# One paced sequence for four token mixers in a decoder block on one Trainium2 core

## The chip, the cores and the metric

The kernel runs on one core of one Trainium2 chip. The metric is the device time of one execution in microseconds (us), given as the median of the runs. The engines are named as the profile names them: PE (TensorE, matrix products; PEld is its weight load), DVE (VectorE), ACT (ScalarE), POOL (GpSimd) and SP (SyncE). In this kernel POOL and SP do little but issue transfers.

## The reference

One decoder layer over 2048 positions of width 1024, float32. A condition vector gives shifts, scales and gates. The first sub-layer projects the normalised input once, feeds two groups of mixers with the result, joins their outputs in one projection and adds it to the residual. The second sub-layer is a feed-forward with a causal convolution of width 3.

```python
sh1, sc1, g1, sh2, sc2, g2 = jnp.split(silu(c) @ w_ada + b_ada, 6)
h = rms_norm(x, norm1_g) * (1 + sc1) + sh1
gq, gk, gv, gr, glr, aq, ak, av = split(h @ w_in)
y_gla = gla_group(gq, gk, gv, log_a, gr, gla_norm_g)        # 4 heads, chunked, a running state
y_att = dilated_attention_group(qa, ka, av)                 # 8 heads, (window, dilation) = (128,1), (512,4), (2048,16)
x = x + g1 * (concat([y_gla, y_att]) @ w_out)
h = rms_norm(x, norm2_g) * (1 + sc2) + sh2
u_gate, u_val = split(causal_depthwise_conv(h @ w_up) + conv_b)
x = x + g2 * ((silu(u_gate) * u_val) @ w_down)
```

## The kernel before

The 2048 positions are four chunks of 512 (`NCH = 4`, `T = 512`). A chunk passes through four pieces of work. `proj(c)` is the input projection; its results go to DRAM scratch. `mix(c)` reads them back and runs the mixers: `gla(c, 0)` and `gla(c, 1)`, then `attn(c, hp)` for four pairs of heads, hp = 0 to 3. `outproj(c)` reads the mixers' output, projects it and computes the second norm. `ffn(c)` is the feed-forward: 44 blocks of the up-projection, and the down-projection in groups of four feature tiles.

Every dense product is made of triples of matmuls (`mm3`, L306 to L308), because each float32 operand is split into a high and a low part. They write to a pool of four PSUM banks called `psg`. The mixers, and every small product of the other pieces (the norms' sums at L442 and L445, the q and k norms at L500 and L501, the gate at L612 and L624), write to a second pool of four banks called `psa`. A weight block is loaded into `wraw` by POOL, rounded by ACT (L240) and its remainder taken by DVE (L241).

The code of one attention pair (two heads, L830 to L972), in the order of its steps, is: scores of dilation 16 (PE L865, biased and reduced to a maximum by DVE L836), scores of dilations 4 and 1 (PE L830, DVE L836), 24 exponentials (ACT L840, after their negated maximum by DVE L855), a weighing of the three branches in some fifteen small DVE operations with two small products (PE L897 and L921), scaling of the probabilities (DVE L917 and L928), 40 transposes on PE (L850) that ACT (L181) and DVE (L183) copy out, products with the values (PE L949 and L954), a last scaling (DVE L934), a transpose back (PE L969), a copy (ACT L971), a sum (DVE L972) and the store. One pair follows the other: the next begins at L865 behind the L969 of the pair ahead. The tiles `kt`, `kw` and `v16` of a pair share two buffers, so the next pair's `kw` is loaded once L949 has read `v16`.

Each piece is a Python generator that yields after a step. `beside(a, na, b, nb)` runs through b and, after each step of b, as many steps of a as keep the share na/nb. `along` does the same and yields, `chain` joins generators. `mix(c)` has 68 steps. `gemm` is the projection of all chunks together with the late part of the condition's product (`ada_late`). This writing order gives each instruction its priority. The scheduler then orders every engine's instructions by priority and by when they can start in its own timeline, and hands out a pool's banks in the order in which the code asks for them.

In the second half of an `outproj(c)`, after its eight blocks and the norm's sum, stands `self.tail`: the last group of the down-projection of the chunk ahead (for chunk 0, the last block of the projection of chunk 3). It is dense work for PE while the second norm is applied.

Of the kernel before, what the change touches and what calls it, by code (L numbers as in the profile page):

```python
# [21 lines left out]
NCH = 4  # L22
# [78 lines left out]
def beside(a, na, b, nb):  # L101

    acc = 0.0
    done = object()
    for _ in b:
        acc += na / nb
        while acc >= 1.0:
            acc -= 1.0
            if next(a, done) is done:
                acc = -1e9  # L110
    for _ in a:
        pass


def along(a, na, b, nb):

    acc = 0.0
    done = object()
    for _ in b:
        acc += na / nb  # L120
        while acc >= 1.0:
            acc -= 1.0
            if next(a, done) is done:
                acc = -1e9
        yield
    for _ in a:
        pass


def chain(*gs):  # L130
    for g in gs:
        yield from g


class K:
# [945 lines left out]
    def run(self):  # L1081
        self.ada_setup()
        self.scratch()
        self.x1, self.h2, self.tail = {}, {}, ()
        self.planned = False
        xs = self.load_x(0)
        acc = None
        for k in range(5):
            acc = self.square(acc, xs[k])
        sqs = [self.tmp.tile([P, T], F32, name="sq", bufs=3) for _ in range(5, KD)]  # L1090
        for sq, x in zip(sqs, xs[5:]):
            self.nc.scalar.activation(sq, x, AF.Square)
        rstd = {0: self.norm_end(acc, more=sqs)}
        h0, ws, done = [], {}, {b: self.pg() for b in FIRST}
        spare = self.at.tile([P, 2048], F32R, name="w0", tag="kt", bufs=2)
        ring = self.at.tile([P, 2048], F32, name="ring", tag="kt", bufs=2)
        for k in range(KD):
            big = [self.at.tile([P, 1024], F32, name="wada", tag="big", bufs=4)]
            pair = [self.gp.tile([P, T], F32, name="wada", tag=t) for t in ("ghi", "glo")] if k < 5 else [ring[:, (k - 5) * 1024:(k - 4) * 1024] if k < 7 else self.at.tile([P, 1024], F32, name="wada", tag="v4", bufs=1)]
            gs = [self.ada(KD + k, big), self.ada(k, pair)]  # L1100
            for g in gs:
                next(g)
            if k < len(FIRST):
                b = FIRST[k]
                ws[b] = self.wblock(self.A["w_ch"][b], KD, P, spare if k == 3 else None)
            for g in gs:
                next(g, None)
            if k == GATE:
                self.gate_ins = self.last
            h0.append(self.norm_mod1(xs[k], k, rstd[0], self.G1, self.mod[:, 0:8]))  # L1110
        for b in FIRST:
            for k in range(KD):
                self.mm3(done[b], ws[b][k:k + 1], h0[k:k + 1], k == 0, True)
        self.consts()

        def src(c):
            def f(k):
                t = self.tmp.tile([P, T], F32, name="sq", bufs=3)
                ld = self.dq.dma_start(t, self.A["xT"][c, k])
                if c == 1:  # L1120
                    self.after(ld)
                return t
            return f

        self.wleft, self.wready, self.wpos = list(self.plan()), [], 0
        self.planned = True
        hs = [h0]

        def begin(c):
            hs.append(self.norm_mod(src(c), rstd[c], self.G1, self.mod[:, 0:8]))  # L1130

        def proj(c):
            yield from self.proj(c, hs.pop(), (lambda: begin(c + 1)) if c < 3 else None, () if c else done)

        def stats(c):

            acc = None
            xs = [src(c)(0)]
            yield
            for k in range(KD):  # L1140
                if k + 1 < KD:
                    xs.append(src(c)(k + 1))
                yield
                acc = self.square(acc, xs[k], xs[k])
            yield
            rstd[c] = self.norm_end(acc, split=True)
            yield

        def ahead(c):

            return along(stats(c), 11, proj(c - 1), 18)

        gemm = along(self.ada_late(), 66, chain(ahead(1), ahead(2), ahead(3), proj(3)), 94)
        for _ in range(27):
            next(gemm)
        beside(self.mix(0), 68, gemm, 72)
        beside(self.mix(1), 68, chain(self.outproj(0), self.ffn(0)), 90)
        beside(self.mix(2), 68, chain(self.outproj(1), self.ffn(1)), 86)
        beside(self.mix(3), 68, chain(self.outproj(2), self.ffn(2)), 90)
        for _ in chain(self.outproj(3), self.ffn(3)):  # L1160
            pass


# [59 lines left out]
```

## Time and profile before

| what | us |
|---|---|
| median of 2 runs | 2602.16 |
| the runs | 2600.97 and 2603.35 |
| span of the profiled execution | 2603.1 |
| first mixer's first DVE step (L663) | 184.0 |
| first eviction of the output projection (L1005), chunks 0 to 3 | 689.7, 1197.9, 1697.8, 2199.5 |
| end of `attn(c, 3)` (L972 starts), chunks 0 to 3 | 663.9, 1160.8, 1635.6, 2153.6 |

The profiled execution's span is within the range of the runs' times. The stages follow from the third and fourth entries: until 184 us start and the projection of chunk 0; until 690 us the rest of the projection with the mixers of chunk 0; then three stages of output projection and feed-forward, each with the mixers of the next chunk; and from 2200 us the last chunk's, with no mixers beside it.

A busy share of PE counts a matmul from its start to its modelled end. Matmuls overlap, so a share near 100% says that PE never stood empty for long, and the rate is read from the spacing of starts.

### The profile page before, as it was taken

Reading aid. Unit: us, or ns where it says so; the run is one execution under the profiler, and the core shown is the slowest. Engines: PE = TensorE matmul, PEld = TensorE weight load, DVE = VectorE, ACT = ScalarE, POOL = GpSimd, SP = SyncE. Lnnn points to the kernel's source line nnn. Section 1 sums busy time; section 2 is a strip of 40 time slices with the busy share of each in tenths; the row PEclk is TensorE's granted clock in tenths of the full one; section 3 lists DMA queues with packets and bytes.
Section 4 is the critical chain, followed back from the end, with each engine's and each line's share of the span. In section 5 each row is a group of like instructions: output and inputs, shape, how many; then the busy total and the mean of one; then the engine's idle time right before and its main releaser. Section 6 shows DMA issues by size and latency. Waiting matters only on the chain.

```text
span 2603.1 us, 46834 instructions
## 1 busy us (share of the span) xinstructions
PE 2559.7 (98%) x18142; PEld 2104.0 (81%) x18142; DVE 1930.2 (74%) x4091; ACT 1277.7 (49%) x2626; POOL 444.4 (17%) x816
## 2 busy tenths in 40 slices
PE   5999999999999999999999999999999999999999
PEld 4888888788788888887788888878888888788887
DVE  7578877768788777777987777689777775766665
ACT  4566556656454444454545544346445453433332
POOL 1343332313210000012100000310000003100001
PEclk8999999999999999999999999999999999999999
DMA  8766675756633344455334344733443435432322
GB/s 291 242 226 234 211 236 170 239 167 201 230 108 100 123 128 122 127 174 199 123 96 139 117 134 136 252 131 114 129 140 127 143 103 189 150 103 97 96 96 84
DMA packets 164194, 405.13 MB, mean 156 GB/s; under 512 B 19154, under 2 KB 61956, under 8 KB 162692
## 3 DMA queue, kind: packets, MB, share of 16 engines
q0 software_dynamic: 88128, 308.59, 35.5%
q1 hardware_dynamic: 75844, 93.55, 11.6%
q8 instruction: 143, 2.34, 0.4%
q14 instruction: 79, 0.65, 0.1%
HBM read 339.15 MB, written 62.91 MB: 154 GB/s over the span
## 4 chain that ended last, share of the span: by engine, by line
PE 77%; issue 1%; DVE 1%; DMA 1%; ACT 0%; POOL 0%; POOLq 0%; DVEq 0%; ACTq 0%
PE psg L306 22%; PE psg L307 22%; PE psg L308 22%; PE psa L850 2%; PE psa L830 2%; PE psa L954 2%; PE psa L680 1%; PE psa L949 1%; PE psa L865 0%; PE psa L753 0%; PE psa L752 0%; PE psa L969 0%; DMA wada<-in_w_ada_dram 0%; PE psa L757 0%; PE psa L779 0%
## 5 line engine op out<-in xcount | busy, mean ns | idle before, releaser
L306 PE MATMUL psg<-hhi,whi 128*128 128x512 f32 x1992 | 782.0, 396 | 9.2 <-ACT hhi L467 5.3
L307 PE MATMUL psg<-hlo,whi 128*128 128x512 f32 x1992 | 782.9, 394 | 6.7 <-DVE hlo L469 6.5
L308 PE MATMUL psg<-hhi,wlo 128*128 128x512 f32 x1992 | 780.2, 392 | 0.7 <-DVE wlo L241 0.7
L240 ACT CAST whi<-wraw 128x1024 fp32r<-128x1024 f32 (+1 forms) x391 | 410.4, 1051 | 467.4 <-PE psg L307 363.2
L241 DVE TENSOR_TENSOR wlo<-wraw,whi 128x1024 fp32r<-128x1024 f32 (+1 forms) x391 | 478.0, 1223 | 187.2 <-ACT whi L240 181.5
L306 PEld LDWEIGHTS psg<-hhi,whi 128*128 128x128 f32 x1992 | 375.0, 189 | 95.2 <-ACT hhi L467 9.3
L307 PEld LDWEIGHTS psg<-hlo,whi 128*128 128x128 f32 x1992 | 375.3, 188 | 86.7 <-DVE hlo L469 9.6
L308 PEld LDWEIGHTS psg<-hhi,wlo 128*128 128x128 f32 x1992 | 375.5, 188 | 80.6 <-issue 1.7
L306 PE MATMUL psg<-ghi,whi 128*128 128x512 f32 x744 | 295.1, 398 | 0.0
L307 PE MATMUL psg<-glo,whi 128*128 128x512 f32 x744 | 292.1, 393 | 0.5 <-DVE glo L999 0.5
L308 PE MATMUL psg<-ghi,wlo 128*128 128x512 f32 x744 | 291.6, 392 | 0.0
L234 POOL DMA_DIRECT2D wraw<-in_w_up_dram x176 | 93.6, 532 | 982.6 <-DVE wlo L241 850.5
L1073 DVE SCALAR_TENSOR_TENSOR x<-psg,mod,x 128x512 f32<-128x512 f32 x192 | 143.2, 749 | 118.2 <-PE psg L308 115.7
L306 PE MATMUL psg<-whi,hhi 128*128 128x512 f32 (+2 forms) x512 | 172.8, 345 | 8.3 <-ACT stg L523 6.2
L308 PE MATMUL psg<-whi,hlo 128*128 128x512 f32 (+2 forms) x512 | 174.8, 345 | 0.0
L307 PE MATMUL psg<-wlo,hhi 128*128 128x512 f32 (+2 forms) x512 | 174.6, 343 | 0.1
L306 PEld LDWEIGHTS psg<-ghi,whi 128*128 128x128 f32 x744 | 139.5, 188 | 34.0 <-issue 5.3
L307 PEld LDWEIGHTS psg<-glo,whi 128*128 128x128 f32 x744 | 139.8, 188 | 30.0 <-issue 1.9
L308 PEld LDWEIGHTS psg<-ghi,wlo 128*128 128x128 f32 x744 | 139.7, 188 | 29.5 <-issue 0.7
L840 ACT ACTIVATE big<-big,nm 128x256 f32<-128x256 f32 (+1 forms) x256 | 122.4, 480 | 33.6 <-DVE nm L855 33.4
L1028 ACT ACTIVATE y<-psg,tables_sb 128x512 f32<-128x512 f32 x176 | 136.1, 776 | 4.5 <-PE psg L308 3.2
L1029 DVE SCALAR_TENSOR_TENSOR y<-psg,tables_sb,y 128x511 f32<-128x511 f32 x176 | 130.7, 743 | 3.7 <-ACT y L1028 3.6
(253 smaller groups left out, 3621.9 us busy)
## 6 DMA issues: line engine op xcount, KB each, us to landing
wraw<-in_w_up_dram POOLq DMA_DIRECT2D x176, 512.0 KB, 3.6
wraw<-in_w_down_dram POOLq DMA_DIRECT2D x88, 512.0 KB, 3.6
wraw<-in_w_ch_dram POOLq DMA_DIRECT2D x44, 512.0 KB, 4.3
v<-v SPq DMA_DIRECT2D x68, 256.0 KB, 5.6
wada<-in_w_ada_dram POOLq DMA_DIRECT2D x64, 256.0 KB, 4.8
wraw<-in_w_tokw_dram POOLq DMA_DIRECT2D x32, 512.0 KB, 4.2
wraw<-in_w_out_dram POOLq DMA_DIRECT2D x32, 512.0 KB, 4.7
sq<-in_xT_dram POOLq DMA_DIRECT2D x48, 256.0 KB, 4.9
```

The lines of the kernel that those rows point to most:

```text
L234: self.dq.dma_start(raw[:, :n], src)
L240: nc.scalar.copy(hi[:, :n], raw[:, :n])
L241: nc.vector.tensor_tensor(lo[:, :n], raw[:, :n], hi[:, :n].bitcast(F32), op=ALU.subtract)
L306: nc.tensor.matmul(ps, wh, hh, start=first and k == 0, stop=False, skip_group_check=shared)
L307: nc.tensor.matmul(ps, wh, hl, start=False, stop=False, skip_group_check=shared)
L308: self.lastmm = nc.tensor.matmul(ps, wl, hh, start=False, stop=k == n - 1, skip_group_check=shared)
L830: nc.tensor.matmul(at(i, hh, z), q[H[hh], i * P:(i + 1) * P], key(H[hh], i, z), start=True, stop=True, skip_group_check=True)
L840: nc.scalar.activation(t[:, lo:hi], t[:, lo:hi], AF.Exp, bias=nm[:, hh, g, i:i + 1], scale=2.0 ** -(h + 1), accum_out=dn[:, hh, g, i:i + 1])
L850: nc.tensor.transpose(ps[:n, i * P:(i + 1) * P], part(S[hh], i), self.C("id"))
L1028: nc.scalar.activation(y, ps, AF.Identity, bias=self.cb[:, b:b + 1], scale=self.cw[:, 2, b:b + 1])
L1029: nc.vector.scalar_tensor_tensor(y[:, 1:], ps[:, :T - 1], self.cw[:, 1, b:b + 1], y[:, 1:], op0=ALU.mult, op1=ALU.add)
L1073: nc.vector.scalar_tensor_tensor(x1, ps, self.mod[:, 40 + cb:41 + cb], x1, op0=ALU.mult, op1=ALU.add)
```

## The change

Before, each chunk's mixers ran beside a piece of dense work of their own: those of chunk 0 beside the rest of the projection, and those of chunk c+1 beside the output projection and feed-forward of chunk c, with 68 steps to 72, 90, 86 and 90. Now the 272 steps of all four chunks' mixers are one sequence, written beside the rest of the projection and the output projection and feed-forward of chunk 0, with 272 steps to 157. Behind it, the output projections and feed-forwards of chunks 1, 2 and 3 are written without any mixers. No instruction is added or removed.

```diff
         for _ in range(27):
             next(gemm)
-        beside(self.mix(0), 68, gemm, 72)
-        beside(self.mix(1), 68, chain(self.outproj(0), self.ffn(0)), 90)
-        beside(self.mix(2), 68, chain(self.outproj(1), self.ffn(1)), 86)
-        beside(self.mix(3), 68, chain(self.outproj(2), self.ffn(2)), 90)
-        for _ in chain(self.outproj(3), self.ffn(3)):
+        beside(chain(*(self.mix(c) for c in range(NCH))), 272, chain(gemm, self.outproj(0), self.ffn(0)), 157)
+        for _ in chain(self.outproj(1), self.ffn(1), self.outproj(2), self.ffn(2), self.outproj(3), self.ffn(3)):
             pass
```

The scheduler's order decides what this does to each engine. The first place is the end of the last attention pair, `attn(3, 3)`, on PE. Names with `psg` are dense products, names with `psa` are the mixers' and the norm's. Before, the end of that pair stands between dense triples of the feed-forward of chunk 2:

```order
L850 MATMUL psa<-consts_sb,big 128x128 x4
L306 MATMUL psg<-hhi,whi 128x512
L307 MATMUL psg<-hlo,whi 128x512
L308 MATMUL psg<-hhi,wlo 128x512
L949 MATMUL psa<-v_21968,s_21923 32x64 x16
L949 MATMUL psa<-v_21968,s_21924 32x64 x16
L954 MATMUL psa<-big,v_22097 64x4x32 x16
L954 MATMUL psa<-big,v_21878 64x8x16 x16
L969 MATMUL psa<-consts_sb,pt 128x128 x4
L306 MATMUL psg<-hhi,whi 128x512
```

Now no dense row stands in the whole pair, nor in the pair ahead of it, and the sum of the second norm of chunk 1 (L445) stands behind both:

```order
L897 MATMUL psa<-xm,consts_sb 128x64
L850 MATMUL psa<-consts_sb,s_15939 128x128 x4
L850 MATMUL psa<-consts_sb,s_15940 128x128 x4
L921 MATMUL psa<-xm,consts_sb 128x32
L850 MATMUL psa<-consts_sb,big 128x128 x32
L949 MATMUL psa<-v_15984,s_15939 32x64 x16
L949 MATMUL psa<-v_15984,s_15940 32x64 x16
L954 MATMUL psa<-big,v_16071 64x4x32 x16
L954 MATMUL psa<-big,v_15918 64x8x16 x16
L969 MATMUL psa<-consts_sb,pt 128x128 x4
L445 MATMUL psa<-rstd,ones 128x512
L306 MATMUL psg<-hhi,whi 128x512 x4
```

What moved is the dense work: counted in dense matmuls between the L969 of one pair and the next, there were 212 to 252 for each of the last three pairs of a chunk's mixers before (chunks 1 to 3); for `attn(3, 1)` there are now 119, for `attn(3, 2)` and `attn(3, 3)` none. The feed-forward of chunk 1 begins behind the last mixer, and 5,136 of the 9,792 dense matmuls stand behind it.

The second place is DVE at the same end. Before, the last pair's evictions (L183, L934, L972) stand between the feed-forward's weight remainders (L241) and convolution (L1029 to L1045):

```order
L183 COPY big<-psa 128x4x128
L241 TENSOR_TENSOR wlo<-wraw,whi 128x1024
L1029 SCALAR_TENSOR_TENSOR y_22474<-psg,tables_sb,y_22474 128x511
L1032 SCALAR_TENSOR_TENSOR y_22474<-halo,tables_sb,y_22474 128x1
L934 TENSOR_TENSOR pt<-psa,f 128x512
L1030 SCALAR_TENSOR_TENSOR y_22474<-psg,tables_sb,y_22474 128x510
L1033 SCALAR_TENSOR_TENSOR y_22474<-halo,tables_sb,y_22474 128x2
L1040 SCALAR_TENSOR_TENSOR th<-th,y_22474 128x512
L972 TENSOR_TENSOR stage<-psa,stage 128x16x32
```

Now the pair has DVE to itself, and behind it come the eight tiles of the second norm (L465, L469):

```order
L917 TENSOR_SCALAR big<-big,f 128x256 x8
L923 TENSOR_TENSOR xm<-psa,consts_sb 128x32
L924 TENSOR_REDUCE f<-xm 128x2x4
L928 TENSOR_SCALAR big<-big,f 128x256 x8
L183 COPY big<-psa 128x4x128 x4
L934 TENSOR_TENSOR pt<-psa,f 128x512
L972 TENSOR_TENSOR stage<-psa,stage 128x16x32
L465 SCALAR_TENSOR_TENSOR sq<-x,G_111,rstd 128x512 x3
L469 SCALAR_TENSOR_TENSOR hlo<-sq,mod,hhi 128x512 x2
```

The third place is PE at `attn(1, 2)`, from the weighing of its branches (L921) on. Before, its transposes (L850) alternate with the up-projection of chunk 0:

```order
L306 MATMUL psg<-hhi,whi 128x512
L921 MATMUL psa<-xm,consts_sb 128x32
L850 MATMUL psa<-consts_sb,big 128x128 x12
L307 MATMUL psg<-hlo,whi 128x512
L308 MATMUL psg<-hhi,wlo 128x512
```

Now the pair runs where the projection of chunk 3 ends, without a dense row until its L969. The sums of the projection's last norm of q or k (L500, L501) stand in the middle of its transposes, and the dense rows that follow (`ghi`) belong to the output projection of chunk 0:

```order
L921 MATMUL psa<-xm,consts_sb 128x32
L850 MATMUL psa<-consts_sb,big 128x128 x16
L500 MATMUL psa<-sqr,blk 128x512
L501 MATMUL psa<-sqr,blk 128x512
L850 MATMUL psa<-consts_sb,big 128x128 x16
L949 MATMUL psa<-v_8619,s_8574 32x64 x16
L949 MATMUL psa<-v_8619,s_8575 32x64 x16
L954 MATMUL psa<-big,v_8741 64x4x32 x16
L954 MATMUL psa<-big,v_8510 64x8x16 x16
L969 MATMUL psa<-consts_sb,pt 128x128 x4
L306 MATMUL psg<-ghi,whi 128x512
```

What moved is again the dense work. Between the L969 of one pair and that of the next there are 42 dense matmuls for `attn(0, 2)`, 128 for `attn(1, 0)` and 48 for `attn(1, 2)` now; before, 234, 239 and 252 (the counts of first pairs run from the last transposes of the gated linear attention, L779). PE passes between dense rows and other rows 669 times before and 503 times now.

## The prediction

> **What bounds the kernel now.** I read the page first, its busy times and its slices.
>
> ```profile
> PE 2559.7 (98%) x18142; PEld 2104.0 (81%) x18142; DVE 1930.2 (74%) x4091; ACT 1277.7 (49%) x2626; POOL 444.4 (17%) x816
> DVE  7578877768788777777987777689777775766665
> PEclk8999999999999999999999999999999999999999
> ```
>
> PE is busy throughout, DVE between 0.6 and 0.9. Then the busy time by stage (busy us of PE, PEld, DVE, ACT and POOL, then granted clock, DMA share and GB/s), cut at the marks of the table above:
>
> ```profile
> 184.00:690.00 506.00, 501.26 (x4155) 419.65 (x4154) 395.71 (x922) 309.76 (x672) 162.31 (x289) 1.00 0.65 216
> 690.00:1198.00 508.00, 508.00 (x3814) 415.87 (x3813) 377.94 (x796) 245.44 (x553) 57.75 (x108) 1.00 0.41 133
> 1198.00:1698.00 500.00, 497.55 (x3840) 405.79 (x3839) 385.75 (x887) 241.67 (x546) 60.92 (x114) 1.00 0.44 142
> 2200.00:2603.10 403.10, 396.16 (x1734) 325.92 (x1732) 263.35 (x402) 145.63 (x180) 48.10 (x90) 0.99 0.32 105
> ```
>
> The same view for the `psa` products alone:
>
> ```profile
> 1198.00:1698.00 500.00, 95.46 (x2070) 80.34 (x2070) 71.58 (x192) 26.06 (x74) 1.00 0.44 142
> ```
>
> A stage with mixers is about 100 us longer than the last, which has none, and the mixers' products keep PE busy for 95 us of it. So PE is the bound in every stage, and the mixers cost their own PE work and little else: everything they wait for is hidden behind dense matmuls. That cover is what the change redistributes.
>
> **Engine sums do not decide.** Since no instruction is added or removed, PE's sum stays. The packed stretch (184 us to the end of the feed-forward of chunk 0) takes over the mixers of two more chunks. On PE it would need 506 + 508 + 2 x 100 = 1214 us. One chunk's mixers put 385.75 - 263.35 = 122 us on DVE and 241.67 - 145.63 = 96 us on ACT, so DVE would have 396 + 378 + 245 = 1019 us (84%) and ACT 748 us (62%). No engine is full on average. What decides is how fast the one chain of mixer steps can go, and whether PE has dense rows while it waits for it.
>
> **Rate of that chain.** The ends of two successive pairs, `attn(2, 0)` and `attn(2, 1)`:
>
> ```profile
> 1436.94 1.07 DVE L972 TENSOR_TENSOR stage<-psa,stage 128x512 f32<-128x512 f32 x1 [0.77 <-ACT stage L971]
> ...
> 1501.08 1.06 DVE L972 TENSOR_TENSOR stage<-psa,stage 128x512 f32<-128x512 f32 x1 [2.88 <-ACT stage L971]
> ```
>
> A pair takes 64 us there with 212 dense matmuls beside it. Dense matmuls start every 0.227 us (first two rows below), which is 48 us; the other 16 us are the pair's own on PE.
>
> ```profile
> 510.80 0.39 PE L307 MATMUL psg<-wlo,hhi 128*128 128x512 f32 x1
> 511.03 0.39 PE L308 MATMUL psg<-whi,hlo 128*128 128x512 f32 x1
> ...
> 513.59 0.49 PE L306 MATMUL psg<-whi,hhi 128*128 128x512 f32 x1 [1.49 <-ACT stg L550]
> ...
> 515.42 0.63 PE L307 MATMUL psg<-wlo,hhi 128*128 128x512 f32 x1
> 515.85 0.63 PE L308 MATMUL psg<-whi,hlo 128*128 128x512 f32 x1
> ```
>
> Where the new order leaves 143 to 205 dense matmuls per pair, PE has 49 to 63 us of work for each. How long would a pair take with nothing else on the engines? That is a sum along its chain:
>
> ```profile
> L954 PE MATMUL psa<-big,v 128*64 128x128 f32 x944 | 55.1, 274 | 0.0
> L971 ACT COPY stage<-psa 128x512 f32<-128x512 f32 x16 | 16.8, 1052 | 35.7 <-PE psa L969 35.7
> L972 DVE TENSOR_TENSOR stage<-psa,stage 128x512 f32<-128x512 f32 x16 | 17.1, 1067 | 21.6 <-ACT stage L971 20.9 <-DMA kw<-kn 0.8
> L836 DVE CUSTOM_DVE_ANT_0 s<-psa,consts_sb 128x32 f32<-128x32 f32 (+3 forms) x128 | 22.0, 236 | 0.8 <-PE psa L865 0.8
> L840 ACT ACTIVATE s<-s,nm 128x32 f32<-128x32 f32 (+3 forms) x128 | 44.5, 349 | 32.0 <-DVE nm L855 32.0
> L840 ACT ACTIVATE big<-big,nm 128x256 f32<-128x256 f32 (+1 forms) x256 | 122.4, 480 | 33.6 <-DVE nm L855 33.4
> L894 DVE TENSOR_TENSOR xm<-md,consts_sb 128x64 f32<-128x64 f32 x16 | 3.6, 224 | 35.6 <-ACT big L840 33.4 <-ACT halo L1035 2.1
> L917 DVE TENSOR_SCALAR big<-big,f 128x256 f32<-128x256 f32 (+1 forms) x128 | 33.0, 333 | 0.0
> L928 DVE TENSOR_SCALAR big<-big,f 128x256 f32<-128x256 f32 (+1 forms) x128 | 34.6, 345 | 0.3
> L183 DVE COPY big<-psa 128x512 f32<-128x512 f32 (+1 forms) x60 | 40.3, 676 | 5.7 <-PE psa L850 5.6
> ```
>
> From one pair's value products on: L954 55.1/16 = 3.4 us, the transpose back 0.6 (an estimate from the four it has), L971 1.05, L972 1.07 (DVE's order puts it ahead of the next scores), eight maxima of 0.24, 1.9, and the next few with their scale, 0.9: 8.9 us. Then 24 exponentials on ACT, 8 x 0.35 + 16 x 0.48 = 10.5 us. Then the weighing, some fifteen small DVE operations at L894's 0.22, 3.3 us, and a copy, 0.7. Then L917 and L928, eight each, (33.0 + 34.6)/16 = 4.2 us, and four copies L183 of the last transposes, 2.7 us. That is 30.3 us, and some 2.5 us for two dozen hand-overs and L949 (estimate): 33 us. It is an estimate from durations alone; the other bound is the 64 us just read, with all the dense work in the way. I take a value near the lower end because in the rows now at the end (first and second places above) nothing else stands on PE and DVE.
>
> One thing adds to it. After PE waited 1.49 us at 513.59, matmuls start 0.43 us apart instead of 0.227: the granted clock is halved. An uncovered pair leaves PE idle through the exponentials, so its products would run at half the clock; those on the chain (L954, the last transposes, the first scores) are about 5 us and would add 4. I take 37 us for an uncovered pair.
>
> The Trainium skill, "TensorE: Matmul & The Clock Gate", Part 1, says that the clock halves after at least one idle window of about 3.4 us and returns after a busy window of that length. The trace agrees with the return (0.43 us spacing from 514 to 518) but shows the drop after a wait of 1.49 us. By the page the uncovered pairs would pay the same, since their exponentials leave PE 10 us, and the sum stays; by the row, each short wait of (2) can cost 1.7 us more, half of the 3.4 us at half rate, which their upper bound holds.
>
> **The change, part by part.** (1) The end of the mixers. The dense work of chunk 1's output projection and tail runs out when `attn(3, 1)` is at L921. The feed-forward of chunk 1 needs the norm's sum L445, for which the pool gives a bank only behind the last mixer. So PE has: the rest of that pair, 6 us (copies 2.7, products, L928); two uncovered pairs, 74 us; from the last L949 to the first dense matmul the 5 us of L954, L969 and L971, then the norm as the trace has it on ACT and DVE, below: 2237.18 - 2230.29 = 6.9 us, and 2 us more at half clock, together 14 us.
>
> ```profile
> 2230.29 1.28 ACT L447 ACT_TABLE_LOAD   x1
> ...
> 2237.18 0.47 PE L306 MATMUL psg<-hhi,whi 128*128 128x512 f32 x1 [1.46 <-ACT hhi L467]
> ```
>
> In the last stage of before this norm ran beside the tail and left PE 1.46 us of wait; here the tail is used up. The window is 6 + 74 + 14 = 94 us, and 2.3 pairs x 16 = 37 us of it is PE work that was paid before too: **+57 us**. With 30 us a pair it is +43, with 47 us +77.
>
> (2) Earlier stretches where the projection waits for a bank of `psa` in turn and the four of `psg` are full. `attn(0, 2)` has 42 dense matmuls (10 us) and 48 belong to `attn(1, 2)` (11 us); with 14 to 16 us of their own PE has 24 to 27 us for a chain of 33 to 37 us: 10 us lost in each. `attn(1, 0)` has 128, but none until its L897: the maxima and exponentials, 3 + 10.5 and hand-overs, some 16 us, against 5 us of scores: 11 us. Together **+31 us**, from 0 (a chain of 25 us) to 60 (contended).
>
> (3) Elsewhere in the packed stretch DVE carries 84%, and the first pair and the first gated attention of a chunk run beside q and k norms and weight remainders. The slices at 0.8 and 0.9 of DVE cost PE next to nothing before, so I give it **+15 us**, from 0 to 50.
>
> (4) PE passes between dense and other rows 166 times less. A matmul's 0.39 exceeds its spacing of 0.227 by 0.16 us, the most that a pass can cost; half of it, **-13 us**, from 0 to -27.
>
> (5) Transfers: the mixers' loads keep their number and move on SP's queue only, with their own pair; the DMA share is 0.41 to 0.44 where they get denser, and 0.65 beside the projection. I cost them at nothing; the chain of an uncovered pair covers them. If `kw`, loaded behind L949, came late, it would show as a wait of L830 on DMA and is inside the 47 us bound. The three later stages lose 30% of their transfers and DVE work, and PE, at 98% and more there before, gains nothing.
>
> Sum on the profiled span: 2603.1 + 57 + 31 + 15 - 13 = 2693. The median of the runs is 0.9 us under that span, so **2692 us**, 3.5% slower.
>
> **Rivals.** A: the same or faster, not slower. If an uncovered pair ran at its busiest engine (the exponentials, 11 us of ACT, and evictions; some 22 us) rather than along its chain, (1) would be 6 + 44 + 14 - 37 = +27, (2) and (3) nothing, (4) -13: 2617 us, no change that can be told. It turns at about 29 us a pair: (1) +41, (2) +10, (3) +10, (4) -13, just under 2% of 2602. For it: PE ran at full rate before, so the order left the chain slack. Against: the exponentials cannot start before their maxima, nor the scaling before all of them. Chance 0.12.
>
> B: the chain is contended everywhere. If each of the 24 pieces of mixers (16 pairs, 8 gated attentions) ended 6 us later than its dense work lasts, since DVE is at 84% and first in its queue may be a 1.2 us weight remainder, (3) is 24 x 6 = 144 us: 2821 us. For it: the packed pairs have 49 us where they had 64. Against: the two slices of DVE at 9 tenths and the many at 8 were borne before with PE full. Chance 0.08.
>
> C: the clock. If the half clock doubled all 37 us of PE work in the window and some 15 us in the places of (2), 2692 + 52 - 8 (already counted) = 2736 us. For it: the wait at 513.59. Against: most products run while ACT or DVE is the later one. Chance 0.12.
>
> That the mixers would not leave the later feed-forwards is excluded by the order: the last mixer stands ahead of 5,136 dense matmuls.
>
> **How the numbers follow.** The forecast, 2650 to 2735, has 0.68, A 0.12, B 0.08, C 0.12. The range reaches from 2635, with a part of A, to 2765 with C and the upper bounds of (1) and (2), and leaves out B and the rest of A. A change of 2% (52 us) is about what a measurement of this kernel can tell from none: slower by over 2% takes the forecast, B and C, less 0.02 for its lower edge, 0.86; within 2% 0.13; faster 0.01, since nothing here gives more than (4).
>
> **What would show it.** Right: a slice or two of low PE at about 1420 us (the 975 us of dense work ahead, 370 of mixers, 44 of start and 33 of (2) to (4)), with the exponentials on ACT beside it; a gap of some 37 us between the last two L972; a halved clock there; three stages of about 400 us behind it with PE at 98% and more and DVE near 0.65. The norm's part is right if the first dense matmul comes 10 to 14 us behind the last L969. Step (2) is shown by PE waiting around 500 to 750 us. Wrong: PE full at the end of the mixers; or PE waits spread over all pairs (B).

## The result and the profile after

The changed kernel takes 2755.28 us (median of 2 runs, 2753.97 to 2756.59) against 2602.16 before: ratio 1.0589, 95% interval 1.0558 to 1.0619. It is slower by 153 us. The forecast was 2692 us, 63 us less. The time lies above the forecast's own band, 2650 to 2735, and inside the range, 2635 to 2765, by 10 us. The profiled execution has a span of 2754.8 us, 151.7 more than that of before, and the sums below are made against it.

The slices of the page, 69 us each:

```profile
PE 2623.9 (95%) x18142; PEld 2152.9 (78%) x18142; DVE 1943.2 (71%) x4091; ACT 1278.9 (46%) x2624; POOL 443.6 (16%) x816
PE   6999988999889999999998699999999999999999
DVE  7688875796776987669876576666576666676665
PEclk8999998999899999999999799999999999999999
```

Behind the start, PE is below 9 tenths in three places: around 410 us, around 760 us and around 1530 us. The first two lie beside the projection, the third is the end of the mixers. Busy times by stage (PE, PEld, DVE, ACT, POOL, granted clock, DMA share, GB/s):

```profile
184.00:470.00 286.00, 270.85 (x2510) 224.87 (x2509) 219.22 (x566) 159.19 (x394) 77.69 (x139) 0.96 0.57 192
470.00:560.00 90.00, 80.22 (x815) 65.83 (x814) 69.93 (x191) 56.68 (x137) 20.16 (x36) 0.91 0.58 193
...
680.00:850.00 170.00, 149.76 (x1286) 118.65 (x1285) 115.71 (x391) 99.69 (x275) 32.48 (x58) 0.88 0.54 177
...
1488.00:1574.00 86.00, 55.08 (x716) 46.85 (x715) 50.32 (x200) 39.35 (x122) 3.31 (x6) 0.82 0.43 129
1574.00:1955.00 381.00, 380.26 (x1670) 314.21 (x1671) 245.46 (x380) 145.09 (x219) 50.27 (x95) 1.00 0.32 111
1955.00:2355.00 400.00, 398.38 (x1746) 328.36 (x1744) 258.66 (x397) 154.05 (x230) 59.80 (x112) 1.00 0.35 121
```

From 1574 us on the kernel is what the prediction said it would be: PE full, DVE at 0.65, full clock. Everything that was lost was lost before. For the same 18142 matmuls PE's busy time rose by 64 us, from 2559.7 to 2623.9, and its empty time by 87. The window at the end, from PE's order of time:

```profile
1488.19 0.39 PE L308 MATMUL psg<-ghi,wlo 128*128 128x512 f32 x1
1488.42 0.30 PE L921 MATMUL psa<-xm,consts_sb 128*128 128x32 f32 x2
...
1508.86 2.95 PE L830 MATMUL psa<-kw,qn 64*128 64x256 f32 x15
1520.02 0.69 PE L897 MATMUL psa<-xm,consts_sb 128*128 128x64 f32 x2 [8.21 <-DVE xm L894]
...
1566.57 0.66 PE L969 MATMUL psa<-consts_sb,pt 128*128 128x128 f32 x4
1567.06 1.02 PE L445 MATMUL psa<-rstd,ones 128*128 128x512 f32 x2
1573.81 2.08 PE L306 MATMUL psg<-hhi,whi 128*128 128x512 f32 x4 [5.72 <-ACT hhi L467]
```

No dense matmul starts between 1488.19 and 1573.81: 85.6 us. The pair's exponentials alone leave PE 8.21 us with nothing to do. The ends of the pairs, from DVE's order of time:

```profile
454.67 1.07 DVE L972 TENSOR_TENSOR stage<-psa,stage 128x512 f32<-128x512 f32 x1 [3.49 <-ACT stage L971]
492.32 1.09 DVE L972 TENSOR_TENSOR stage<-psa,stage 128x512 f32<-128x512 f32 x1 [1.58 <-DMA kw<-kn]
...
783.08 1.09 DVE L972 TENSOR_TENSOR stage<-psa,stage 128x512 f32<-128x512 f32 x1 [1.43 <-ACT stage L971]
828.60 1.08 DVE L972 TENSOR_TENSOR stage<-psa,stage 128x512 f32<-128x512 f32 x1 [0.25 <-ACT stage L971]
...
1452.03 1.03 DVE L972 TENSOR_TENSOR stage<-psa,stage 128x512 f32<-128x512 f32 x1 [3.29 <-ACT stage L971]
1505.08 1.03 DVE L972 TENSOR_TENSOR stage<-psa,stage 128x512 f32<-128x512 f32 x1 [4.57 <-ACT stage L971]
1536.76 1.01 DVE L972 TENSOR_TENSOR stage<-psa,stage 128x512 f32<-128x512 f32 x1 [4.58 <-ACT stage L971]
1568.31 1.03 DVE L972 TENSOR_TENSOR stage<-psa,stage 128x512 f32<-128x512 f32 x1 [4.55 <-ACT stage L971]
```

The two pairs without dense work take 31.7 and 31.6 us (the last three rows). A pair with dense work beside it takes longer: `attn(0, 2)` 37.7 us, `attn(1, 2)` 45.5, `attn(3, 1)` 53.0.

**Where the 152 us went.** For each of the 24 pieces of mixers (two gated attentions and four pairs per chunk) I take the time from the end of the piece ahead to its own end, less 0.2275 us for each dense matmul of 512 columns that PE's order has there (narrower ones counted by their columns, so `attn(1, 1)`'s 128 rows count as 124). What is left is the piece's own PE work and PE's lost time; its difference to the same piece of before is the loss.

| pieces | loss, us |
|---|---|
| chunks 0 and 1, beside the projection and on to 885 us | +84 |
| of it `attn(0, 2)`, `attn(1, 0)`, `attn(1, 2)` | +12, +22, +19 |
| chunk 2 and chunk 3 to `attn(3, 0)` | +18 |
| `attn(3, 1)`, `attn(3, 2)`, `attn(3, 3)` | +10, +13, +16 |
| behind the last mixer, the norm first | +10 |

A single piece is good to about 1 us, by which of its last instructions is taken as its end.

What a pair loses goes by the dense work that it is given, and not evenly. A bare pair takes 31.6 us, 16 of them PE's own, so dense work could hide in some 16 us of each. What did hide there is 31.6 plus the dense time less the time that the pair took:

| pair | dense matmuls | dense us | pair took us | hidden us |
|---|---|---|---|---|
| `attn(3, 3)` | 0 | 0 | 31.6 | 0 |
| `attn(0, 2)` | 42 | 9.6 | 37.7 | 3.5 |
| `attn(1, 2)` | 48 | 10.9 | 45.5 | -3.0 |
| `attn(3, 1)` | 119 | 27.1 | 53.0 | 5.7 |
| `attn(1, 1)` | 124 | 28.2 | 52.6 | 7.2 |
| `attn(0, 1)` | 126 | 28.7 | 49.2 | 11.1 |
| `attn(2, 3)` | 143 | 32.5 | 55.3 | 8.8 |
| `attn(2, 1)` | 159 | 36.2 | 59.8 | 8.0 |
| `attn(0, 3)` | 168 | 38.2 | 53.7 | 16.1 |
| `attn(2, 2)` | 176 | 40.0 | 59.8 | 11.8 |
| `attn(1, 3)` | 187 | 42.5 | 57.6 | 16.5 |
| before, `attn(2, 1)` | 212 | 48.2 | 64.1 | 15.7 |

So dense work of 27 to 36 us, enough in amount, hides only 6 to 11 us, and the amount alone doesn't decide: 38 us hid 16 in `attn(0, 3)`, 40 us hid 12 in `attn(2, 2)`. Three places show how. In `attn(1, 2)` all of PE's dense rows stand among the scores, before the exponentials, and none behind them:

```profile
783.83 0.65 PE L865 MATMUL psa<-kt,qf 64*32 64x64 f32 x32
...
800.01 1.13 PE L830 MATMUL psa<-kw,qn 64*128 64x256 f32 x4
...
802.34 0.39 PE L308 MATMUL psg<-hhi,wlo 128*128 128x512 f32 x1
808.82 0.69 PE L897 MATMUL psa<-xm,consts_sb 128*128 128x64 f32 x2 [6.10 <-DVE xm L894]
...
816.61 0.78 PE L500 MATMUL psa<-sqr,blk 128*128 128x512 f32 x1
...
825.23 0.47 PE L306 MATMUL psg<-ghi,whi 128*128 128x512 f32 x1
```

From the first half of L865, which starts at 781.21, to L897 it takes 27.6 us; in the bare pair 16.1 (1503.89 to 1520.02). The dense rows lengthened the scores, where the pair's own products were ready and PE in demand, and from 802.34 to 825.23 there was nothing left to fill the holes. In `attn(3, 1)` the chain waits behind other work on DVE between L899 and L913:

```profile
1479.49 0.22 DVE L899 TENSOR_TENSOR xm<-psa,consts_sb 128x64 f32<-128x64 f32 x1
1479.62 0.68 DVE L431 TENSOR_TENSOR rstd<-rstd,sq 128x512 f32<-128x512 f32 x1
...
1484.04 1.23 DVE L241 TENSOR_TENSOR wlo<-wraw,whi 128x1024 fp32r<-128x1024 f32 x1
...
1486.06 0.19 DVE L913 TENSOR_TENSOR xm<-f,consts_sb 128x32 f32<-128x32 f32 x1
```

That is 6.6 us, where the bare pair has 3.0 (1520.75 to 1523.72). On PE the L921 that reads this `xm` starts at 1488.42, behind the last dense rows, and the 15 us from there to the end of L969 have no dense row.

In `attn(1, 0)` no dense matmul starts for 26.5 us. The gate's products (L612, L624) stand among the scores there, with a wait of 3.98 us for a DVE step of the gate:

```profile
681.29 0.39 PE L308 MATMUL psg<-hhi,wlo 128*128 128x512 f32 x1
681.61 0.86 PE L865 MATMUL psa<-kt,qf 64*32 64x64 f32 x64
...
686.99 1.23 PE L624 MATMUL psa<-gw,glr 96*128 96x256 f32 x4 [3.98 <-DVE glr L620]
...
707.81 0.41 PE L306 MATMUL psg<-whi,hhi 128*128 128x256 f32 x1
```

The clock is a part of it too. In these three stretches of `attn(0, 2)`, `attn(1, 0)` and `attn(1, 2)` the granted clock was 0.50 throughout:

```profile
474.30:484.50 10.20, 5.60 (x25) 4.47 (x25) 8.27 (x32) 6.97 (x13) 0.53 (x1) 0.50 0.30 104
685.90:709.80 23.90, 16.01 (x59) 12.24 (x60) 13.94 (x53) 18.90 (x63) 1.94 (x4) 0.50 0.28 90
805.40:819.00 13.60, 8.64 (x37) 7.37 (x38) 8.46 (x32) 5.97 (x20) 0.57 (x2) 0.50 0.25 78
```

PE was busy for 30 us of them. Over the whole trace it was busy for 119 us at half clock, where before it was for 24; ahead of the window, from 184 us on, for 83.

### The profile page after: what moved, and what is told of

Its sections match the earlier page's. It is cut to its first block, busy times and chain, and to the rows that moved or that the text cites. A ratio compares the mean times of both kernels' runs of the same rounds, so it can differ in the third digit from the quotient of the medians.

```text
span 2754.8 us, 46881 instructions
## 1 busy us (share of the span) xinstructions
PE 2623.9 (95%) x18142; PEld 2152.9 (78%) x18142; DVE 1943.2 (71%) x4091; ACT 1278.9 (46%) x2624; POOL 443.6 (16%) x816
## 3 DMA queue, kind: packets, MB, share of 16 engines
q1 hardware_dynamic: 75844, 93.55, 10.9%
## 4 chain that ended last, share of the span: by engine, by line
PE 67%; ACT 3%; DMA 3%; DVE 3%; issue 2%; POOL 0%; SPq 0%; POOLq 0%; ACTq 0%; DVEq 0%
PE psg L306 20%; PE psg L307 20%; PE psg L308 20%; PE psa L850 2%; PE psa L830 1%; ACT big L840 1%; DMA kw<-k 1%; PE psa L680 1%; DMA sq<-y 1%; PE psa L954 1%; DVE wlo L241 0%; PE psa L753 0%; PE psa L752 0%; PE psa L949 0%; ACT s L840 0%
## 5 line engine op out<-in xcount | busy, mean ns | idle before, releaser
L241 DVE TENSOR_TENSOR wlo<-wraw,whi 128x1024 fp32r<-128x1024 f32 (+1 forms) x391 | 478.6, 1225 | 224.2 <-ACT whi L240 216.9
L306 PEld LDWEIGHTS psg<-ghi,whi 128*128 128x128 f32 x744 | 139.8, 188 | 31.7 <-issue 3.0
L836 DVE CUSTOM_DVE_ANT_0 big<-psa,consts_sb 128x256 f32<-128x256 f32 (+1 forms) x256 | 89.3, 400 | 69.5 <-PE psa L830 69.4
```

Of the source, the lines that this page charges most:

```text
L241: nc.vector.tensor_tensor(lo[:, :n], raw[:, :n], hi[:, :n].bitcast(F32), op=ALU.subtract)
L306: nc.tensor.matmul(ps, wh, hh, start=first and k == 0, stop=False, skip_group_check=shared)
L836: TTR = lambda out, i0, i1, acc: nc.vector.tensor_tensor_reduce(out, i0, i1, 1.0, -3.0e38, ALU.add, ALU.max, acc)
```

## The experiments

Theory 1: the projection loses because dense work waits for a bank of `psa` in turn. Theory 2: the chain of a pair is stretched by whatever stands ahead of it, on every engine, so that a pair beside dense work takes 50 to 60 us and loses what its dense work falls short of. The kernel before had a median of 2603.8 to 2604.6 us in the batches. Losses "by piece" are worked out as in the table above.

**e1: the second norm's sum takes its bank from `psg`,** so that the feed-forward of chunk 1 can begin while mixers run.

```diff
-        ms = self.pa()
+        ms = self.pa() if split or more else self.pg()
```

> The changed kernel, with the sum of the second norm (L445) taking its bank from the dense work's pool of PSUM instead of the mixers'; nothing else. The order then keeps dense rows in all of the last three pairs. Theory 1 (the feed-forward of chunk 1 waits for a bank in turn behind the last mixer): the bare window of 85.6 us at the end goes; it held 2.3 pairs x 16 = 37 us of work paid anyway, so 49 us less, with 0 to 15 us given back to pairs that go slower beside dense work: 2706 to 2722 us. Theory 2 (the chain of mixers is too slow for the packed stretch, wherever dense work stands): the wait moves to other places and the time stays within 15 us of 2755.

Measured 2724.87 us, ratio 1.0458 (1.0433 to 1.0482), 30 less than the change. The window is gone: the last three pairs get 140, 210 and 183 dense matmuls and take 50 to 73 us. The time misses the upper end by 3 us: `attn(3, 2)` still loses 6.5 us, and L445 now waits on PE ahead of dense rows. That is the second row; the first is the first norm at the kernel's start, with 11.2 us before as well:

```profile
PE psa L445 <- ACT sq L1092: 10.8, 1, 10.8
PE psg L445 <- DVE rstd L431: 8.9, 3, 3.1
```

(engine, line and tile, releaser: us in total, times, longest). The projection's losses are as in the change, 87 us by `attn(1, 3)`.

**e2: all the norms' and the gate's small sums take banks of `psg`.**

```diff
-        ms = self.pa()
+        ms = self.pg()
...
-        pt = self.pa()
+        pt = self.pg()
...
-            ps = self.pa()
+            ps = self.pg()
```

> As e1, and also the small products of the projection (q and k norms, gate, the first norm's sum) take their banks from the dense work's pool. Theory 1 (small products of the dense work wait in turn behind the mixers): the loss of about 85 us in the ten pieces beside the projection mostly goes too: 2620 to 2650 us. Theory 2 (the chain of mixers is too slow there whatever the banks): little more than e1, 2690 to 2725 us.

Measured 2774.39 us, ratio 1.0654 (1.0632 to 1.0676): slower than the change. Both forecasts fell, and this run doesn't tell why: PE now waits 45.8 us in all at L500 for `sqr`, and each such sum holds one of four banks that the dense work needs. Inconclusive on banks.

**e5: the change's pace beside the projection only,** the rest of the mixers spread over chunks 0 and 1.

```diff
...
+        for _ in gemm:
+            acc += 272 / 157
+            while acc >= 1.0:
+                acc -= 1.0
+                next(mixers)
+        beside(mixers, 147, chain(self.outproj(0), self.ffn(0), self.outproj(1), self.ffn(1)), 176)
...
```

> The changed kernel's order up to the end of the projection (the same counts of dense matmuls per piece for the first eleven pieces); from there the other 147 steps of the mixers are spread over the output projections and feed-forwards of chunks 0 and 1. If the losses add by place, the 85 us of the first eleven pieces stay and the rest goes: 2603 + 85 = 2688, 2680 to 2700 us. If the first losses are only moved work that is won back later: below 2650 us.

Measured 2685.36 us, ratio 1.0317 (1.0301 to 1.0332), in the first range. By piece, +89 us stand at the end of `attn(1, 2)`; the pieces behind `attn(1, 3)`, with 196 dense matmuls or more to each pair, add -5. The losses are made where the order is dense and nowhere else; they add up.

**e6: before's pace beside the projection,** then the three other chunks' mixers beside chunks 0 and 1.

```diff
...
+        beside(self.mix(0), 68, gemm, 72)
+        beside(chain(self.mix(1), self.mix(2), self.mix(3)), 204, chain(self.outproj(0), self.ffn(0), self.outproj(1), self.ffn(1)), 176)
...
```

> The reverse: beside the projection the pace of before (chunk 0's mixers alone), then the other 204 steps over the output projections and feed-forwards of chunks 0 and 1, at 1.16 steps to one, with 120 to 205 dense matmuls per pair; two feed-forwards without mixers. Theory 1 (only dense work that waits for a bank in turn loses): no bare window and no projection wait, 2590 to 2612 us. Theory 2 (a pair beside dense work takes some 55 to 60 us, so pairs with under 170 dense matmuls, 39 us and 16 of their own, lose what is missing): nine such pairs at 2 to 12 us, 2625 to 2660 us.

Measured 2649.61 us, ratio 1.0175 (1.0157 to 1.0192). The projection loses nothing, and behind it the pairs with 149 to 177 dense matmuls take 52 to 60 us and lose up to 7 us each. `attn(2, 2)`, where the sum L445 of chunk 1 stands and only 120 matmuls, loses 19. The time is in theory 2's range, and the other pairs behave as it says. Half of the 38 us lies in that one pair, where no dense matmul starts for 13 us around the sum; whether the sum came late by its bank or by the chain isn't separated there.

**e11 and b11: a bank of their own (`psn`) for the small sums, taken from `psa`,** in the change and in the kernel before.

```diff
-        self.psa = pool("psa", 4, space=PSUM)
+        self.psa = pool("psa", 3, space=PSUM)
+        self.psn = pool("psn", 1, space=PSUM)
...
-        ms = self.pa()
+        ms = self.pn()
...
```

> The changed kernel with psa cut to three banks and one bank of its own (psn) for the sums of the first and second norms, of the q and k norms, and for the gate; psg keeps its four. No such sum waits in turn behind the mixers any more. Theory 1 (the projection's pieces lose their 85 us because dense work waits for a bank in turn behind a pair): they lose less than half of that, and the window at the end closes as it did with the norm's sum in psg, together 2670 to 2700 us. Theory 2 (a pair's chain is drawn out by what stands ahead of it on DVE, ACT and PE, and takes longer than the dense work given to it): the projection's pieces still lose 70 us or more, only the window changes, 2715 to 2750 us.

> The kernel before with the same cut of the banks (psa three, psn one), to price it alone. Both theories: PE stays full, 2600 to 2620 us.

e11 took 2698.46 us, ratio 1.0361 (1.0346 to 1.0376), in the range of theory 1. But the control was not neutral: b11 took 2656.88 us, ratio 1.0203 (1.0188 to 1.0218), some 3 us more in most pairs with three banks, so that the range was hit is luck. Against this control the change costs 42 us instead of 153. The window is gone, and by piece the projection loses 38 us instead of 84. `attn(1, 2)` has 201 dense matmuls now instead of 48; its two ends, from DVE's order of time (L976 is the L972 of this kernel), and PE between them:

```profile
805.31 1.08 DVE L976 TENSOR_TENSOR stage<-psa,stage 128x512 f32<-128x512 f32 x1 [3.98 <-ACT stage L975]
870.64 1.06 DVE L976 TENSOR_TENSOR stage<-psa,stage 128x512 f32<-128x512 f32 x1
```

```profile
804.20:868.60 64.40, 64.40 (x477) 51.31 (x476) 50.71 (x129) 35.73 (x82) 5.30 (x10) 1.00 0.43 134
```

PE is full and at full clock through it: with a bank of its own for the sums the order gives this pair its dense work and it loses nothing, so its loss came from a bank in turn. `attn(0, 2)` and `attn(1, 0)` keep theirs (14 and 19 us over the control): they are given 8 and 131 dense matmuls. There the gate and the q and k norms share the one `psn`, so a wait in turn isn't excluded, and what those two lose isn't separated.

**e13 and b13: the same bank taken from `psg`.**

```diff
-        self.psg = pool("psg", 4, space=PSUM)
+        self.psg = pool("psg", 3, space=PSUM)
...
```

> The changed kernel with a bank of its own (psn) for the norms' and the gate's small sums, taken from psg (three left) and not from psa (four kept). Theory 1 (dense work waiting in turn for a bank of psa makes both the window and half of the projection's loss; the rest is pairs that are given too little dense work): over its own control it loses 35 to 60 us, nothing of it in one window at the end of the mixers, the largest pieces at attn(0, 2), which is given no dense matmul, and attn(1, 0), which is given 112. Theory 2 (the pairs' chain alone, banks without part): over its control it still loses 100 us or more.

> The kernel before with the same cut (psg three, psn one), the control. A bank of psg is filled for 5.5 us (24 matmuls of 0.227) in the projections and 2.7 us in the down-projection and evicted in 0.75 to 1.3 us, so three should nearly do: 2600 to 2635 us by both theories.

e13 took 2758.89 us, ratio 1.0585 (1.0567 to 1.0603), and its control 2677.64, ratio 1.0281 (1.0266 to 1.0296). The difference is 81 us, between the two forecasts, so both missed; the window is gone, as theory 1 said, and the projection loses 62 us over the control. The largest pieces are `attn(0, 2)` and `attn(1, 0)`, 19 and 22 us, as theory 1 named them. `attn(1, 2)`, with 160 dense matmuls, loses 14 here, and not by a bank: PE waits 11.1 us at the pair's first L834 (L830 of the other kernels) for the load of `v`. Both controls missed too: a bank fewer costs the kernel before 52 or 74 us.

**e9 and b9: without the refinement in the q and k norms,** in the change and before.

```diff
-            self.newton(sq, ms, T)
```

> The changed kernel without the refinement of the reciprocal root in the 32 q and k norms (three DVE operations each, 0.75 + 0.69 + 0.69 = 2.1 us a norm, 68 us in all, some 51 of them beside the mixers). It leaves that part of the computation out. Theory 2: DVE ahead of the chain is what draws it out, so a good part of the 51 us comes back in the projection, 2715 to 2740 us. Theory 1 (banks): a norm's sum holds its bank 2 us less, little comes back, 2740 to 2753 us.

> The kernel before without the same refinement, also left out there, as a control. PE is full there, so both theories: 2595 to 2604 us.

e9 took 2726.70 us, ratio 1.0468 (1.0452 to 1.0484), 29 less than the change and in the range of theory 2; b9 took 2593.64, ratio 0.9958 (0.9942 to 0.9975), 11 less than before and below its range of 2595 to 2604. The change thus gains 18 to 20 us more than the control by 51 us less on DVE beside the mixers. By piece that is the projection: 66 us over its control by `attn(1, 3)`, where the change has 84. This part of DVE's work makes a fifth of the loss. What the rest of DVE's work makes no run shows.

**e8: more bare pairs.** Before's pace beside the projection, then all other mixers beside chunk 0.

```diff
...
+        beside(self.mix(0), 68, gemm, 72)
+        beside(chain(self.mix(1), self.mix(2), self.mix(3)), 204, chain(self.outproj(0), self.ffn(0)), 90)
...
```

> Before's pace beside the projection, and the other three chunks' mixers all beside the output projection and feed-forward of chunk 0: five pairs and two gated attentions at the end are left without dense work, where the change left two pairs. If a bare pair takes the 31.7 us of the changed kernel's trace, each of the five costs 31.7 - 16 = 16 us (79), the two gated attentions perhaps 10 each, the pairs ahead some 30 in all, the norm 7: 2720 to 2760 us. With the prediction's 37 us a pair: 2750 to 2790. If a bare pair took the 52 to 60 us that a pair takes beside dense work: 2850 us or more.

Measured 2785.82 us, ratio 1.0696 (1.0680 to 1.0712), 26 over the range for 31.7 us a pair and inside the one for 37 us. So the time alone would speak for 37; the pairs speak for 31.7 (L972 in DVE's order of time, the last of `attn(2, 3)` and the four of chunk 3):

```profile
1385.87 1.05 DVE L972 TENSOR_TENSOR stage<-psa,stage 128x512 f32<-128x512 f32 x1 [0.25 <-ACT stage L971]
1497.50 1.04 DVE L972 TENSOR_TENSOR stage<-psa,stage 128x512 f32<-128x512 f32 x1 [4.59 <-ACT stage L971]
1529.12 1.02 DVE L972 TENSOR_TENSOR stage<-psa,stage 128x512 f32<-128x512 f32 x1 [4.59 <-ACT stage L971]
1560.36 1.02 DVE L972 TENSOR_TENSOR stage<-psa,stage 128x512 f32<-128x512 f32 x1 [4.59 <-ACT stage L971]
1592.51 1.01 DVE L972 TENSOR_TENSOR stage<-psa,stage 128x512 f32<-128x512 f32 x1 [4.55 <-ACT stage L971]
```

The last three take 31.6, 31.2 and 32.2 us, `attn(2, 3)` takes 33.5 and the first pair behind the gated attentions 36.8, and the five bare pairs lose 83 us (79 expected). What is over comes from the rest: the two bare gated attentions take some 38 us each and lose 18 and 25 (10 expected), and the pieces ahead lost 39 instead of 30. The price of a bare pair that follows another pair is settled.

**e10: one sequence at a slower pace.**

```diff
...
+        for _ in gemm:
+            acc += 1.3
+            while acc >= 1.0:
+                acc -= 1.0
+                next(mixers)
+        beside(mixers, 272 - 93, chain(self.outproj(0), self.ffn(0), self.outproj(1), self.ffn(1), self.outproj(2), self.ffn(2)), 266)
...
```

> One sequence at a lower pace: 1.3 steps to each step of the projection's rest (1.73 in the changed kernel), the remaining mixers spread over the output projections and feed-forwards of chunks 0 to 2. Pairs are given 195, 131, 195 and 186 dense matmuls beside the projection and 203 to 372 behind it. If a pair loses what its dense work falls short of, some 200 matmuls for the 52 to 60 us it takes beside dense work, only the second pair loses much, 10 to 20 us: 2605 to 2625 us. If it were the denser mixers as such, by DVE's load, the projection would lose 30 us or more: 2635 us or more.

Measured 2609.96 us, ratio 1.0023 (1.0013 to 1.0033): in the first range. Nothing is lost beside the projection in sum (+6 at the second pair, which has 131 dense matmuls, -8 at the first), and the pieces behind it, with 203 to 372 to a pair, add 9 in sum. One sequence costs next to nothing, the pace costs. No run that keeps the whole computation beats the kernel before, whose PE stands at 98%.

## Why the prediction held in part

**What bounds (held).** PE bounds the kernel, PE's and DVE's instruction counts stayed, and the time was lost where PE lacks dense rows, waiting or at half clock. e10 shows it from the other side: the same sequence with enough dense rows costs 6 us.

**(1) The end of the mixers (right, 8 us too large).** Predicted: a window of 94 us, net +57. It is 85.6 us, less the same 37 us of PE work: +49, as the pieces say (10 + 13 + 16 + 10). On the prediction's own marks (last dense row, L949 to L949, first dense matmul) it is 11 + 63 + 11 where 6 + 74 + 14 were named, so two errors partly cancelled. A bare pair is 31.6 us and not 37: the estimate from durations, 33, was good. At half clock only the weighing's products and the transposes ran, not L954; the windows of `attn(3, 2)`, granted clock in the third column from the end, show where:

```profile
1511.50:1515.40 3.90, 0.31 (x2) 0.00 (x0) 2.13 (x13) 3.90 (x17) 0.00 (x0) 0.99 0.95 209
1515.40:1520.00 4.60, 0.00 (x0) 0.00 (x0) 0.23 (x1) 4.31 (x18) 0.00 (x0) 0.50 0.51 183
1520.00:1529.00 9.00, 7.43 (x33) 6.73 (x34) 7.48 (x30) 1.88 (x4) 0.00 (x0) 0.50 0.00 0
1529.00:1536.70 7.70, 7.70 (x209) 6.87 (x207) 2.74 (x5) 2.19 (x3) 0.00 (x0) 1.00 0.48 125
```

The rest of `attn(3, 1)` took 11 us to the end of L949 instead of 6. The norm was quicker than thought: 6.6 us from the end of the last L969 to the first dense matmul, where 10 to 14 were named. That the norm's bank opens the window is shown by e1, e11 and e13, in which it is gone.

**(2) Three earlier stretches (right in place, too small).** Predicted +31 in `attn(0, 2)`, `attn(1, 0)` and `attn(1, 2)`; measured 12 + 22 + 19 = 53, inside the upper end of 60. The step that failed is the price "24 to 27 us for a chain of 33 to 37 us: 10 us lost in each": it lets all of a pair's dense work hide in its holes. In `attn(1, 2)` none hid, so it lost the whole 16 us of a bare pair and 3 more. In `attn(0, 2)` only 3.5 of 9.6 us hid; that it came out near its 10 us is luck, since the price took a bare chain of 33 to 37 where it is 31.6. In `attn(1, 0)` the stretch without a dense matmul was 26.5 us and not 16: the gate among the scores and the half clock were left out of the sum. The cause that was given, a bank of `psa` in turn, is shown for `attn(1, 2)` by e11. For `attn(0, 2)` and `attn(1, 0)` it stays open.

**(3) Elsewhere (the largest miss).** "+15 us, from 0 to 50", on the ground that DVE's full slices cost nothing before. With (4) that was +2. Measured are 102 us ahead of the window, less 53, so some 49 with (4) inside: at the bound if (4) is nothing, and 62, above it, if (4) is its -13. The slices of before had dense matmuls worth 180 and more of 512 columns beside each pair, and with these PE is full however late the chain is. With 119 to 177 the lateness of the chain counts, and a pair beside dense work takes 50 to 60 us where its PE work is 43 to 56. This is rival B's mechanism. B put 6 us on each of 24 pieces, 144 us for (3) alone; the pieces outside (1) and (2) lost less, and unevenly: `attn(1, 3)` with 187 lost nothing, the pairs with 124 to 176 lost 1 to 10, the two first pairs with 195 lost 5 to 9. Of the 84 us beside the projection, e9 gives at least 18 to DVE's work; banks in turn hold 22 to 46 of it by e13 and e11, each with an order and counts of its own, so these shares don't add up, and the half clock (under rival C) lies across them.

**(4) Fewer passes (not settled).** No piece shows it by itself.

**(5) Transfers (wrong by 13 us at most).** They were costed at nothing. Waits of PE by releaser:

```profile
PE psa L897 <- DVE xm L894: 31.6, 6, 8.2
PE psg L306 <- ACT hhi L467: 13.8, 6, 5.7
PE psa L830 <- DMA kw<-k: 12.7, 8, 3.0
```

The third row is new: `kw`, for which a buffer comes free only behind L949, is late in denser pairs (2.12 us at the start of `attn(3, 1)`). In the bare pairs, which were named as its cover, it cost 0.2 us. The largest, 3.03 us ahead of L830 at 406.45, falls together with a half clock from 406.0 to 419.7, so a late load can cost more than its own wait.

**Rival A** (22 us a bare pair) is out by the 31.6 of five pairs and more. **Rival C** is out for the bare pairs: the half clock held for 13.6 us of one, but the products in it stretched the pair by 3 to 4 us at most (eight transposes 1.91 us instead of 1.04, 32 in 5.97 instead of some 4). Elsewhere it is not out. Its 15 us of products in the places of (2) are there: PE was busy for 30 us at half clock in them. Ahead of the window it was for 83 us in all, where the stages of before had 3.4; half of the difference, some 40 of the 102 us lost there, is the most that the doubling itself can have cost (an estimate). Where DVE or ACT was later anyway it cost nothing, and no run changed the clock alone, so its share stays open.

**The range.** It reached 2765 for the upper bounds of (1) and (2) and for C, and left out B. The excess came from (2), (3) and in part the clock, with B's mechanism at less than half of B's price, so that the range holds the time is partly luck.

## What to carry to other kernels

When an order is packed, don't price a stretch as the longer of the chain and PE's work: dense rows hide a chain's wait only if they stand directly ahead of the waiting product in PE's order, as they didn't in `attn(1, 2)`. So take the bare chain plus the dense work as the high estimate (`attn(1, 2)` took 3 us more even) and the longer of the bare chain and PE's whole work as the low one. Here pairs with 187 or more dense matmuls (43 us, nearly three times the 16 us of holes) mostly lost next to nothing, but 168 covered `attn(0, 3)` and 195 left 5 to 9 us open in the first pairs of chunks 0 and 3. A pool that serves both a long chain and another stage's small sums ties the two together in the order of the code; look for such a sum before you move either.

## What was not expected of the hardware

The granted clock fell to half 3.6 us behind the last product (1511.8 to 1515.4), and came back at 1529.0, 5 us after the last wait (1.55 us, until 1523.97). The Trainium skill, "TensorE: Matmul & The Clock Gate", Part 1, gives an idle window of about 3.4 us for the fall and a busy one for the return. These two agree with it, but other falls in this trace do not: a wait of 1.46 us, until 1981.75, was followed by dense matmuls 0.43 us apart from 1983.6 to 1986.2, as 1.49 us was in the kernel before. So here a wait of less than half that length was enough for a fall. The mean granted clock is 0.971 where before it was 0.994.

At half speed that is 2 x 0.029 x 2755 = 160 us in the clock's lower state, against some 31 before: five times as long. In the bare pairs it cost little, as shown above; ahead of the window some 40 us is the estimate of its upper bound. And a single PSUM bank of eight is worth 2.0% (b11) or 2.8% (b13) to a kernel whose PE shows 97 to 98% busy either way; in b13 the granted clock fell from 0.994 to 0.982, which a busy share doesn't show.
